# Two sets of PSUM banks for the FFNs' output projections, the attention's weight ring carried on into w_out, and FFN 2's two plain tiles taken block by block: a decoder layer in fp32 on one core

## Chip, cores and metric

The kernel runs on one core of a Trainium2 chip. The metric is the device time of one execution in microseconds (us). Five engines work side by side, each through its own list of instructions in order: TensorE (PE: matmul; PEld is its weight load), VectorE (DVE), ScalarE (ACT), GpSimd (POOL) and SyncE (SP), which here only issues loads. Matmuls write to PSUM, of which there are eight banks; DVE and ACT read the banks out.

## The reference, cut to what matters

One layer for 1024 prompt rows and 32 sample rows (8 sequences of 4), all in fp32, D = 1024, D_FF = 2816:

```python
x = x + 0.5 * gate1 * swiglu_ffn(mod(norm(x)), ffn1_w_in, ffn1_w_out)
x = x + gate2 * (sig(g_A) * DiffAttn(h) + sig(g_B) * Retention(h)) @ w_out     # h = mod(norm(x))
x = x + 0.5 * gate3 * swiglu_ffn(mod(norm(x)), ffn2_w_in, ffn2_w_out)
y = rms_norm(x)
# swiglu_ffn(h, w_in, w_out): a, b = split(h @ w_in);  (silu(a) * b) @ w_out
```

The outputs are y, the keys and values of the attention, and the retention states. Keys, values and states of the sample rows' past are read from a paged cache.

## The kernel before

**Layout.** x lies transposed in SBUF, eight tiles (k = 0 to 7) of 128 features by 1056 rows. The rows go in three blocks of 352 (`RB`; block index `rb`); the last block ends with the 32 sample rows. An fp32 product is made of three matmuls (`mm3`, L239 to L244): each operand is split into a rounded part h, by ACT (L183), and a rest l, by DVE (L193) or, where `eng` is `G`, by POOL (L191); then h·h (L242), h·l (L243) and l·h (L244) are added in one bank. hh[k] and hl[k] are the two parts of the normed, modulated x; a "unit" (`unit_g`, L246) is one 128-column tile of a weight times one block of rows: 8 x 3 matmuls into one bank.

**Weights.** Class `W` (L200) is a ring: `raw` tiles for what is loaded (`load`, by SP), and `parts` pairs of h and l tiles (`out`). `get` (L218) loads, takes a pair and splits. A load waits until the last reader of its raw tile is done, a split until the last matmul on its pair.

**PSUM.** `psum(mm, aux, big)` (L130) hands out the banks: with (3, 3, 1) three banks rotate under the tag "mm" (`mm_ps`, the units), three under "aux" (`aux_ps`), and a double one is "big".

**What sets the order.** The program is written as generators that are woven together (`weave`, L268, with `step` tying a side step behind the main matmul named last). A planner then sorts each engine's instructions before the run, by its own estimate of when each is ready, the earlier in the program first; on the chip an engine goes through its list in that order. Loads stand in SP's list, stores and some loads in POOL's.

**The stages**, in order of time: FFN 1 in (two forms, below), FFN 1 out, retention, differential attention with gates, w_out, FFN 2 in, FFN 2 out with the last norm.

*FFN in.* The first column tiles of w_in are done plainly (`ffn_plain`, L484): for each tile and block a unit for a and one for b, silu by ACT, a product by DVE (L500), a store of the gate product to `gd`. The order is written out at L488: `lead` tiles go together, block by block. FFN 1 has three plain tiles with lead 2, FFN 2 two with lead 1. After block (0, 0) FFN 2 runs `final()` (L1553): the norm of the third block (L438 to L465), which writes hh and hl, then the closing of pools and the room for the sums. From then on `sums` (L514) makes sums of quarters of hh and hl on DVE and ACT. The other tiles take seven products instead of eight (`ffn_seven`, L548) on 4 x 4 blocks of h and w_in; their weights are loaded two tiles of 128 columns at a time, and sums of them are split ahead, at most five (`AHEAD`) before use. FFN 1 uses the ring `W(lower, 2, 4)` (L732) for all of this and for its projection, FFN 2 the ring `w3 = W(last, 3, 3)` (L1529).

*FFN out* (`ffn_out`, L632). w_out's rows go in chunks of two or four 128-row tiles; for each, output tile o and block rb, `one` (L659) multiplies into a bank and DVE adds the result to x (the residual, L475; L480 and L482 for the sample rows). In the last chunk the block is the outer loop (L686), and each block, once done, is normed (`after1`, L809, with `rsqrt_s`, L356, whose sums take an "aux" bank) or, in FFN 2, normed, transposed and stored (`after2`, L1566, whose tiles ym and yt take "mm" banks). In FFN 1 the first units of the retention follow.

*Attention and w_out.* From L1223 on the weights of the attention and of the gates go through `w = W(left, 2, 2, G)`, opened behind the pool "gates" and closed with it. `to_wout` (L1462) runs the gates of head 7 (two weights, three blocks: six units), writes the merged branches to `md`, closes the pools (L1479), opens `w2 = W(xs2, 2, 3)` in their place and a tile for x, loads x again, and does the units of w_out for blocks 0 and 1, woven with `da_sample` (L1073), the attention of the sample rows. The third block of w_out, which needs the sample rows, follows in the loop at L1540, with two norms in between (L1547).

Of the kernel before, what the change touches and what calls it, by code (L numbers as in the profile page):

```python
# [20 lines left out]
P = 128  # L21
# [84 lines left out]
def build(tc, i):  # L106
    nc = tc.nc
    V, S, T, G = nc.vector, nc.scalar, nc.tensor, nc.gpsimd
# [39 lines left out]
    def aux_ps(name):  # L148
        return banks[0][1].tile([P, 512], F32, tag="aux", name=name, bufs=banks[0][3])
# [136 lines left out]
    with tc.tile_pool(name="init", bufs=1) as ip:  # L286
        vec = ip.tile([P, P], F32, name="vec")
        o = 0
# [343 lines left out]
    def ffn_out(w, tp, x, wout, gt, after, chunks, reload, bridge=iter(()), more=iter(())):  # L632


        def parts(t, ci, q):
            return t[(4 if ci % 2 == 0 else 0) + q]

        def stage(ci):
            for q, ft in enumerate(chunks[ci]):
                if ci == 0:  # L640
                    for c in range(2):
                        r = w.p.tile([P, 8, P], F32, tag="wr", name=f"gr{ft}{c}", bufs=w.raw)[:].rearrange("p k c -> p (k c)")[:, :HR]
                        ld(out=r, in_=gd[ft][:, c * HR:(c + 1) * HR])
                        split(*half(4 + 2 * q + c, 0), r)
                else:
                    r = tp.tile([P, ROWS], F32, tag="gr", name=f"gr{ft}", bufs=2)
                    ld(out=r[:], in_=gd[ft][:, :])
                    split(parts(hh, ci, q)[:], parts(hl, ci, q)[:], r[:])
                yield

        assert len(chunks[0]) == 2
        run(stage(0))
        for ci, fs in enumerate(chunks):
            f0, nf = fs[0], len(fs)
            cw = 1024 // nf
            rows = wout[f0 * P:(f0 + nf) * P, :]
            nxt = stage(ci + 1) if ci + 1 < len(chunks) else iter(())

            def one(wt, o, rb):  # L659
                p_ = aux_ps(f"po{ci}_{o}_{rb}")  # L660
                cc = (o * P) % cw
                ws = [(wt[0][:, q, cc:cc + P], wt[1][:, q, cc:cc + P]) for q in range(nf)]
                if ci == 0:
                    c, s = divmod(rb, 2)
                    mm3(p_[:, :QR], ws, [tuple(t[4 + 2 * q + c][:, s * QR:(s + 1) * QR] for t in (hh, hl)) for q in range(nf)])
                    residual_at(tp, x, o, rb * QR, QR, p_, gt())
                else:
                    mm3(p_[:, :RB], ws, [tuple(parts(t, ci, q)[:, rbs(rb)] for t in (hh, hl)) for q in range(nf)])
                    residual(tp, x, o, rb, p_, gt())

            if ci < len(chunks) - 1:
                for ct in range(nf):
                    step(more)
                    wt = w.get(rows[:, ct * cw:(ct + 1) * cw], nf, cw, f"wo{ci}_{ct}")
                    if ci == 0 and ct == 0:
                        reload()
                    for o in range(ct * cw // P, (ct + 1) * cw // P):
                        for rb in range(4 if ci == 0 else NRB):
                            one(wt, o, rb)
                        if o % 2:  # L680
                            next(nxt, None)
                run(nxt)
            else:
                wts = [w.get(rows[:, ct * cw:(ct + 1) * cw], nf, cw, f"wo{ci}_{ct}") for ct in range(nf)]
                todo = iter(())
                for rb in range(NRB):  # L686
                    for o in range(KT):
                        one(wts[o * P // cw], o, rb)
                        if rb == NRB - 1 and o == BO:
                            step(bridge)  # L690
                        if o == 2:
                            step(todo)
                    if rb == NRB - 1:
                        run(bridge)
                    todo = after(tp, rb)
                    next(todo)
                run(todo)
# [34 lines left out]
    w = W(lower, 2, 4)  # L732
    bridge = []
    with ExitStack() as sc, ExitStack() as sb_:
# [28 lines left out]
        w2 = W(sc, 1, 1)  # L763
# [456 lines left out]
                               scalar=subg[:], in1=rr, op0=ALU.mult, op1=ALU.mult)  # L1220


    with ExitStack() as left, ExitStack() as right:  # L1223
        gp = pool(left, "gates")
        w = W(left, 2, 2, G)
        up = pool(left, "dau")
        cosd = up.tile([P, ROWS], F32, name="cosd")
        sind = up.tile([P, ROWS], F32, name="sind")
# [230 lines left out]
        right.close()  # L1459
        psum(3, 3, 1)  # L1460

        def to_wout():  # L1462
            def merged(n0, n1):
                for n_ in range(n0, n1):
                    rb, k = divmod(n_, KT // 2)
                    n = SC if rb == NRB - 1 else RB
                    rc = slice(rb * RB, rb * RB + n)
                    for j in range(2):
                        split(hh[2 * k + j][:, rc], hl[2 * k + j][:, rc], ms[n_][:, j, :n])
                    if len(ms) < NRB * KT // 2:  # L1470
                        mload()

            w.eng = WE
            for n, _ in enumerate(gates(7)):
                if n in MC:
                    merged(MC.index(n), MC.index(n) + 1)
                yield
            merged(len(MC), 4)
            left.close()  # L1479
            w2 = W(xs2, 2, 3)  # L1480
            xp = pool(xs2, "x2")
            X = xp.tile([P, KT, ROWS], F32, name="Y")
            x.extend(X[:, k, :] for k in range(KT))
# [13 lines left out]
            for o in range(1, KT):  # L1497
                order += [(o, 0), (o - 1, 1)]
            for j, (o, rb) in enumerate(order + [(KT - 1, 1)]):
                if rb == 0:  # L1500
                    ws[o] = w2.get(w_out[:, o * P:(o + 1) * P], 8, P, f"wo{o}")
                p_ = yield from unit_g(ws[o], rb, f"wop{o}_{rb}")
                residual(None, x, o, rb, p_, mods[5])
                yield
                if j in (0, 8):
                    merged(4 if j == 0 else 8, 8 if j == 0 else 12)
                if j in XL:
                    xload(XL.index(j) + 1, p_[:, :1])
# [16 lines left out]
            mload()  # L1525
        weave(to_wout(), da_sample(sd), RATIO)
        sx.close()
        X, w = wo
        w3 = W(last, 3, 3, side="right")  # L1529
        tp2 = pool(last, "t2", side="right")  # L1530
        tp = pool(tail, "wo", side="right")
        V.tensor_tensor(out=ors[:], in0=ors[:], in1=gbs[:], op=ALU.mult)
# [7 lines left out]
        for n, o in enumerate((5, 6, 7, 0, 1, 2, 3, 4)):  # L1540
            if n > 2:
                w.eng = G if n in NG else None
                ws[o] = w.get(w_out[:, o * P:(o + 1) * P], 8, P, f"wo2{o}")
            p_ = unit(ws[o], 2, f"wop{o}_2")
            residual(tp, x, o, 2, p_, mods[5])
            if n in (NN, NN + 2):
                run(norm(tp, X, (n - NN) // 2, mods, 7, 6))  # L1547
                keep((n - NN) // 2)
# [4 lines left out]
        def final():  # L1553
            yield from norm(tp, X, 2, mods, 7, 6)
            keep(2)
            tail.close()
            xs2.close()
            gx.extend(quarters(xs3))
            gx.append(pool(tas, "ta", side="right"))


    with last:
        with ExitStack() as s2:
# [39 lines left out]

            todo = back()
            win2 = i["ffn2_w_in"][0]
            ffn_plain(w3, tp2, win2, [0, 1], 1, {(0, 0): final()}, todo)
            for _ in todo:
                pass
            psum(0, 0, 1, True)
# [43 lines left out]
```

## Time and profile before

| | us |
|---|---|
| runs, median of 3 (lowest to highest) | 3100.89 (3099.73 to 3101.14) |
| the profiled execution, its own time | 3098.73 |
| its span, first to last instruction | 3097.0 |
| PE busy | 2963.5 |
| DVE busy | 1969.6 |
| ACT busy | 1319.7 |
| mean granted clock of PE | 0.986 of full speed |

Times of single instructions and waits are read from the one profiled execution, from the start of its span. In it the stages lie about so: FFN 1 in to 585, its projection to 872, retention and attention to 2170, w_out to 2342, FFN 2 in to 2812, its projection to the end. A matmul's duration is modelled; matmuls overlap, so the step from one start to the next is what a stream of them costs. An engine's idle time counts only where the end depends on it.

### The profile page before, as it was taken

Reading aid. Unit: us, or ns where it says so; the run is one execution under the profiler, and the core shown is the slowest. Engines: PE = TensorE matmul, PEld = TensorE weight load, DVE = VectorE, ACT = ScalarE, POOL = GpSimd, SP = SyncE. Lnnn points to the kernel's source line nnn. Section 1 sums busy time; section 2 is a strip of 40 time slices with the busy share of each in tenths; the row PEclk is TensorE's granted clock in tenths of the full one; section 3 lists DMA queues with packets and bytes.
Section 4 is the critical chain, followed back from the end, with each engine's and each line's share of the span. In section 5 each row is a group of like instructions: output and inputs, shape, how many; then the busy total and the mean of one; then the engine's idle time right before and its main releaser. Section 6 shows DMA issues by size and latency. Waiting matters only on the chain.

```text
span 3097.0 us, 51415 instructions
## 1 busy us (share of the span) xinstructions
PE 2963.5 (96%) x20167; PEld 2831.4 (91%) x20167; DVE 1969.6 (64%) x3823; ACT 1319.7 (43%) x2580; POOL 542.6 (18%) x722
## 2 busy tenths in 40 slices
PE   6999999999999999999999999998998999999998
PEld 2899999999999999988899999987898999999998
DVE  4875666665566666667667777665558655556547
ACT  5554444422234343346556556544444433333112
POOL 2200000000132322312233332332023000000002
PEclk8999999999999999999999999999999999999999
DMA  7144343643121322223222121225641222226321
GB/s 278 52 134 121 116 121 119 217 153 114 65 90 62 103 78 81 91 73 114 67 67 64 60 80 57 76 74 171 204 151 47 76 83 76 77 74 218 97 63 57
DMA packets 278732, 319.29 MB, mean 103 GB/s; under 512 B 15568, under 2 KB 224049, under 8 KB 278490
## 3 DMA queue, kind: packets, MB, share of 16 engines
q1 hardware_dynamic: 253418, 232.83, 24.5%
q0 software_dynamic: 25072, 83.18, 7.4%
q8 instruction: 158, 2.59, 0.4%
q14 instruction: 84, 0.69, 0.1%
HBM read 240.00 MB, written 75.96 MB: 102 GB/s over the span
## 4 chain that ended last, share of the span: by engine, by line
PE 33%; DVE 9%; issue 4%; DMA 4%; ACT 3%; POOL 2%; ACTq 0%; DVEq 0%; POOLq 0%; SPq 0%
PE x L244 3%; PE x L242 2%; PE x L243 2%; PE po L242 2%; PE po L243 2%; PE po L244 2%; DVE mx L1328 1%; PE q L242 1%; PE q L243 1%; PE q L244 1%; PE gp L242 1%; ACT P L1330 1%; PE gp L244 1%; PE gp L243 1%; DMA gr<-gd 1%
## 5 line engine op out<-in xcount | busy, mean ns | idle before, releaser
L242 PE MATMUL x<-hh,c 128*128 128x264 f32 x624 | 179.0, 287 | 2.6 <-ACT hh L183 1.6
L244 PE MATMUL x<-hh,c 128*128 128x264 f32 x624 | 178.2, 286 | 1.5 <-DVE c L193 1.5
L243 PE MATMUL x<-hl,c 128*128 128x264 f32 x624 | 179.0, 287 | 0.2 <-DVE hl L193 0.2
L193 DVE TENSOR_TENSOR c<-s,c 128x512 fp32r<-128x512 f32 x156 | 107.7, 691 | 111.4 <-ACT c L183 108.5
L242 PE MATMUL x<-gh,c 128*128 128x264 f32 x624 | 178.2, 286 | 0.0
L243 PE MATMUL x<-gl,c 128*128 128x264 f32 x624 | 177.6, 285 | 0.0
L244 PE MATMUL x<-gh,c 128*128 128x264 f32 x624 | 177.3, 284 | 0.0
L1330 ACT ACTIVATE P<-s,mx 128x256 f32<-128x256 f32 (+7 forms) x128 | 94.2, 739 | 138.4 <-DVE mx L1328 127.6
L475 DVE SCALAR_TENSOR_TENSOR Z<-po,mod,Z 128x352 f32<-128x352 f32 (+3 forms) x176 | 96.5, 554 | 83.7 <-PE po L244 83.3
L475 DVE SCALAR_TENSOR_TENSOR X<-po,mod,X 128x352 f32<-128x352 f32 (+3 forms) x152 | 83.0, 551 | 89.2 <-PE po L244 89.2
L625 POOL DMA_DIRECT2D gd<-p x39 | 21.2, 543 | 649.0 <-DVE p L620 649.0
L242 PEld LDWEIGHTS x<-hh,c 128*128 128x128 f32 x624 | 118.7, 190 | 3.8 <-ACT hh L183 1.8
L244 PEld LDWEIGHTS x<-hh,c 128*128 128x128 f32 x624 | 118.8, 191 | 1.8 <-DVE c L193 1.7
L242 PEld LDWEIGHTS x<-gh,c 128*128 128x128 f32 x624 | 117.4, 188 | 2.4
L243 PEld LDWEIGHTS x<-hl,c 128*128 128x128 f32 x624 | 118.6, 190 | 0.5 <-DVE hl L193 0.4
L243 PEld LDWEIGHTS x<-gl,c 128*128 128x128 f32 x624 | 117.3, 188 | 0.9
L244 PEld LDWEIGHTS x<-gh,c 128*128 128x128 f32 x624 | 117.4, 188 | 0.2
L183 ACT ACTIVATE c<-s 128x512 fp32r<-128x512 f32 x156 | 97.6, 626 | 42.1 <-PE y L244 24.5
L242 PE MATMUL po<-hh,wo_0h 128*128 128x352 f32 (+1 forms) x328 | 104.5, 319 | 4.9 <-DVE X L475 4.7
L242 PE MATMUL po<-hh,wo_1h 128*128 128x352 f32 (+1 forms) x328 | 104.8, 320 | 2.9 <-DVE rs L480 1.2
L183 ACT ACTIVATE hh<-gr 128x1056 fp32r<-128x1056 f32 (+1 forms) x48 | 47.5, 1010 | 133.5 <-DMA gr<-gd 66.8
L243 PE MATMUL po<-hl,wo_0h 128*128 128x352 f32 (+1 forms) x328 | 103.7, 316 | 0.0
(1445 smaller groups left out, 11187.2 us busy)
## 6 DMA issues: line engine op xcount, KB each, us to landing
gr<-gd SPq DMA_DIRECT2D x40, 528.0 KB
gd<-u POOLq DMA_DIRECT2D x39, 264.0 KB, 2.6
gd<-p POOLq DMA_DIRECT2D x39, 264.0 KB, 2.3
ada_0r<-ada_w SPq DMA_DIRECT2D x18, 512.0 KB
ada_1r<-ada_w SPq DMA_DIRECT2D x18, 512.0 KB
ada_2r<-ada_w SPq DMA_DIRECT2D x18, 512.0 KB
ada_3r<-ada_w SPq DMA_DIRECT2D x18, 512.0 KB
st<-state_ret SPq DMA_DIRECT2D x32, 256.0 KB
```

The costliest lines, as they stand in the source:

```text
L183: S.activation(out, in_, AF.Copy, scale=scale)
L193: (eng or V).tensor_tensor(out=l, in0=src, in1=f(h), op=ALU.subtract)
L242: T.matmul(out, wh, xh, start=first and j == 0, stop=False, **kw)
L243: T.matmul(out, wh, xl, start=False, stop=False, **kw)
L244: behind[0] = T.matmul(out, wl_, xh, start=False, stop=last and j == n - 1, **kw).ins
L475: V.scalar_tensor_tensor(out=x[k][:, c0:c0 + n], in0=p_[:, :n], scalar=gt[:, k, 0:1], in1=x[k][:, c0:c0 + n], op0=ALU.mult, op1=ALU.add)
L625: st(out=gd[ft][:, :HR], in_=p1[:])
L1328: V.tensor_reduce(out=mx[:, :n], in_=sv[:, :, :wd], op=ALU.max, axis=AX.X, negate=True)
L1330: S.activation(pr[c][:, :wd], sv[:, j, :wd], AF.Exp, bias=mx[:, j:j + 1], accum_out=sums[c][:, qb:qb + 1])
```

## The change

`one` takes an "mm" bank for odd o and an "aux" bank for even o, in both FFNs. The ring w of the attention is opened ahead of the pool "gates", so that it lies below it, and is closed only in `final()`. Its tiles serve w_out: the first weight is loaded and split at step 9 of the last head's gates, and each later one by a new function `column`, which takes its raw tile from w and its pair from w, or for every third from w2, now a ring of no raw tile and one pair. w3 has two raw tiles and four pairs in place of three and three, and FFN 2's plain tiles go with lead 2: (tile, block) = (0,0), (1,0), (0,1), (1,1), (0,2), (1,2).

```diff
@@ -657,7 +657,7 @@
             nxt = stage(ci + 1) if ci + 1 < len(chunks) else iter(())
 
             def one(wt, o, rb):
-                p_ = aux_ps(f"po{ci}_{o}_{rb}")
+                p_ = (mm_ps if o % 2 else aux_ps)(f"po{ci}_{o}_{rb}")
                 cc = (o * P) % cw
                 ws = [(wt[0][:, q, cc:cc + P], wt[1][:, q, cc:cc + P]) for q in range(nf)]
                 if ci == 0:
@@ -1220,9 +1220,10 @@
                                scalar=subg[:], in1=rr, op0=ALU.mult, op1=ALU.mult)
 
 
+    ring = ExitStack()
+    w = W(ring, 2, 2, G)
     with ExitStack() as left, ExitStack() as right:
         gp = pool(left, "gates")
-        w = W(left, 2, 2, G)
         up = pool(left, "dau")
         cosd = up.tile([P, ROWS], F32, name="cosd")
         sind = up.tile([P, ROWS], F32, name="sind")
@@ -1459,6 +1460,13 @@
         right.close()
         psum(3, 3, 1)
 
+        def column(o, n, name):
+
+            raw = w.load(w_out[:, o * P:(o + 1) * P], 8, P, name)
+            h, l = (wo[1] if n % 3 == 2 else w).out(8, P, name)
+            split(h[:], l[:], raw[:], eng=w.eng)
+            return h, l
+
         def to_wout():
             def merged(n0, n1):
                 for n_ in range(n0, n1):
@@ -1474,10 +1482,12 @@
             for n, _ in enumerate(gates(7)):
                 if n in MC:
                     merged(MC.index(n), MC.index(n) + 1)
+                if n == 9:
+                    ws[0] = w.get(w_out[:, :P], 8, P, "wo0")
                 yield
             merged(len(MC), 4)
             left.close()
-            w2 = W(xs2, 2, 3)
+            w2 = W(xs2, 0, 1)
             xp = pool(xs2, "x2")
             X = xp.tile([P, KT, ROWS], F32, name="Y")
             x.extend(X[:, k, :] for k in range(KT))
@@ -1497,8 +1507,8 @@
             for o in range(1, KT):
                 order += [(o, 0), (o - 1, 1)]
             for j, (o, rb) in enumerate(order + [(KT - 1, 1)]):
-                if rb == 0:
-                    ws[o] = w2.get(w_out[:, o * P:(o + 1) * P], 8, P, f"wo{o}")
+                if rb == 0 and o:
+                    ws[o] = column(o, o, f"wo{o}")
                 p_ = yield from unit_g(ws[o], rb, f"wop{o}_{rb}")
                 residual(None, x, o, rb, p_, mods[5])
                 yield
@@ -1525,8 +1535,8 @@
             mload()
         weave(to_wout(), da_sample(sd), RATIO)
         sx.close()
-        X, w = wo
-        w3 = W(last, 3, 3, side="right")
+        X = wo[0]
+        w3 = W(last, 2, 4, side="right")
         tp2 = pool(last, "t2", side="right")
         tp = pool(tail, "wo", side="right")
         V.tensor_tensor(out=ors[:], in0=ors[:], in1=gbs[:], op=ALU.mult)
@@ -1540,7 +1550,7 @@
         for n, o in enumerate((5, 6, 7, 0, 1, 2, 3, 4)):
             if n > 2:
                 w.eng = G if n in NG else None
-                ws[o] = w.get(w_out[:, o * P:(o + 1) * P], 8, P, f"wo2{o}")
+                ws[o] = column(o, n - 1, f"wo2{o}")
             p_ = unit(ws[o], 2, f"wop{o}_2")
             residual(tp, x, o, 2, p_, mods[5])
             if n in (NN, NN + 2):
@@ -1555,6 +1565,7 @@
             keep(2)
             tail.close()
             xs2.close()
+            ring.close()
             gx.extend(quarters(xs3))
             gx.append(pool(tas, "ta", side="right"))
 
@@ -1603,7 +1614,7 @@
 
             todo = back()
             win2 = i["ffn2_w_in"][0]
-            ffn_plain(w3, tp2, win2, [0, 1], 1, {(0, 0): final()}, todo)
+            ffn_plain(w3, tp2, win2, [0, 1], 2, {(0, 0): final()}, todo)
             for _ in todo:
                 pass
             psum(0, 0, 1, True)
```

## Rows read from the trace of the kernel before

**Rows 1.** The page, its first line and part 1: busy time of each engine, its share of the span, and instructions.

```profile
span 3097.0 us, 51415 instructions
PE 2963.5 (96%) x20167; PEld 2831.4 (91%) x20167; DVE 1969.6 (64%) x3823; ACT 1319.7 (43%) x2580; POOL 542.6 (18%) x722
```

**Rows 2.** The table of engines by stretch: start and end of the stretch, its length, busy us of PE, PEld, DVE, ACT and POOL (with instructions), granted clock of PE, share and rate of the DMAs. The second half of the last chunks of FFN 1's output projection; the end of the gates and the start of w_out; the seven products of FFN 2.

```profile
810.00:872.00 62.00, 55.69 (x328) 53.59 (x327) 42.63 (x80) 29.84 (x58) 19.92 (x20) 0.97 0.23 76
2179.00:2198.00 19.00, 13.59 (x64) 12.11 (x63) 9.13 (x23) 8.16 (x20) 0.71 (x1) 0.73 0.77 244
2430.00:2812.00 382.00, 382.00 (x3131) 382.00 (x3130) 204.56 (x390) 149.58 (x321) 20.08 (x37) 1.00 0.27 84
```

**Rows 3.** The timeline of DVE in FFN 1's last chunk: start, us, engine, line, operation, out<-in, count. L456 is the norm's, L475 the residual, L436 the norm's sum of squares.

```profile
835.25 2.26 DVE L456 SCALAR_TENSOR_TENSOR nt<-X,mod,rrn 128x352 f32<-128x352 f32 x3
...
843.26 1.56 DVE L475 SCALAR_TENSOR_TENSOR X<-po,mod,X 128x352 f32<-128x352 f32 x3
...
848.03 0.52 DVE L436 TENSOR_TENSOR acc<-acc,sq 128x352 f32<-128x352 f32 x1
```

**Rows 4.** Who PE waited for from 585 to 872 us (FFN 1's output projection): us in total, times, longest us.

```profile
PE po L242 <- DVE X L475: 4.7, 2, 4.2
PE po L242 <- DVE rs L480: 2.0, 2, 1.3
PE rsn L359 <- POOL acc L436: 0.8, 1, 0.8
```

**Rows 5.** The table of engines by stretch, columns as in rows 2, for three pieces with a lowered clock.

```profile
843.50:846.90 3.40, 3.01 (x10) 3.01 (x11) 2.44 (x5) 1.85 (x4) 2.34 (x3) 0.50 0.33 121
...
2181.50:2184.90 3.40, 3.40 (x16) 3.26 (x15) 0.73 (x2) 0.85 (x2) 0.71 (x1) 0.50 1.02 295
...
2188.40:2195.10 6.70, 5.76 (x22) 5.12 (x23) 3.56 (x8) 2.66 (x6) 0.00 (x0) 0.50 0.74 230
```

**Rows 6.** The timeline of PE, its last matmuls for the gates.

```profile
2169.84 0.32 PE L243 MATMUL gp<-hl,g_0h 128*128 128x352 f32 x1
2170.00 0.32 PE L244 MATMUL gp<-hh,g_0l 128*128 128x352 f32 x1
```

**Rows 7.** Who PE waited for from 2812 to 3057 us (FFN 2's output projection).

```profile
PE po L242 <- DVE Z L475: 1.3, 3, 0.6
PE po L242 <- DVE rs L480: 0.4, 1, 0.4
```

**Rows 8.** Who PE waited for from 3057 to 3097 us (the tail).

```profile
PE yt L1588 <- ACT yo L1591: 2.2, 3, 1.8
```

**Rows 9.** What writes or reads the tile wo0r: engine, operation, count, ns min/median/max, first and last start.

```profile
L211 SPq DMA_DIRECT2D wo0r<-w_out x1: 395/395/395, 2181.2 to 2181.2; - x1
L183 ACT ACTIVATE wo0h<-wo0r x1: 1041/1041/1041, 2187.9 to 2187.9; 128x1024 fp32r<-128x1024 f32 x1
L193 DVE TENSOR_TENSOR wo0l<-wo0r,wo0h x1: 1226/1226/1226, 2189.0 to 2189.0; 128x1024 fp32r<-128x1024 f32 x1
```

**Rows 10.** The timeline of SP, which issues loads: start, us to issue, line, out<-in, count.

```profile
2179.15 0.33 SPq L1126 DMA_DIRECT2D vp<-cache_v  x1
...
2181.83 0.42 SPq L1126 DMA_DIRECT2D vp<-cache_v  x1
```

**Rows 11.** Who PE waited for from 2170 to 2300 us (w_out and the sample attention).

```profile
PE wop L242 <- ACT wo0h L183: 3.0, 1, 3.0
PE kpt L1132 <- DMA kp<-cache_k: 2.1, 1, 2.1
PE spa L1152 <- DVE sdm L1148: 1.1, 3, 0.5
PE wop L244 <- DVE wo0l L193: 0.3, 1, 0.3
```

**Rows 12.** Who PE waited for from 2341 to 2430 us (FFN 2's plain tiles and the first seven products).

```profile
PE pa L243 <- POOL hl L462: 3.0, 2, 2.4
PE x L242 <- ACT hh L183: 1.6, 1, 1.6
PE x L244 <- DVE c L193: 1.5, 1, 1.5
PE x L242 <- DVE silu L500: 0.7, 1, 0.7
```

**Rows 13.** The timeline of DVE around the last norm before FFN 2. L436 is its sum of squares, L519 and L520 are sums for the seven products, L193 is a split.

```profile
2349.78 0.53 DVE L436 TENSOR_TENSOR acc<-acc,sq 128x352 f32<-128x352 f32 x1 [2.73 <-ACT sq L435]
...
2364.09 0.69 DVE L519 TENSOR_TENSOR t<-hh 128x528 f32<-128x528 f32 x1
2364.71 0.70 DVE L520 TENSOR_TENSOR t_0u<-hl 128x528 f32<-128x528 f32 x1
...
2369.03 1.23 DVE L193 TENSOR_TENSOR wb1l<-wb1r,wb1h 128x1024 fp32r<-128x1024 f32 x1 [2.39 <-ACT wb1h L183]
```

**Rows 14.** The timeline of SP, one of FFN 2's first loads.

```profile
2291.51 0.37 SPq L211 DMA_DIRECT2D wb1r<-ffn_w_in  x1
```

**Rows 15.** The timeline of DVE, in w_out's third block.

```profile
2303.39 0.58 DVE L475 SCALAR_TENSOR_TENSOR Y<-wop,mod,Y 128x352 f32<-128x352 f32 x1 [3.23 <-PE wop L244]
```

**Rows 16.** The table of engines by stretch, columns as in rows 2, for the seven products of FFN 1.

```profile
195.00:585.00 390.00, 390.00 (x3083) 374.11 (x3083) 231.76 (x405) 177.73 (x363) 18.43 (x34) 1.00 0.40 123
```

**Rows 17.** The timeline of DVE, in the first tiles of FFN 2's seven products. L572 is a sum of weight blocks.

```profile
2423.45 0.69 DVE L572 TENSOR_TENSOR s<-wa4r 128x512 f32<-128x512 f32 x1 [0.25 <-DMA wa4r<-ffn_w_in]
```

## The prediction, made before the changed kernel ran

> **What bounds it now.** I read the page first: TensorE (PE) is busy for 2963.5 of 3097.0 us [rows 1], so only its idle time, and time at a low clock, can be won; VectorE (DVE) at 64% matters where it makes PE wait. Next the table of engines by stretch [rows 2]: both seven-product stretches of the FFNs leave PE no gap (FFN 2's: 382.00 of 382.00), while PE is idle for 6.3 us of the end of FFN 1's output projection, for 5.4 us (at a mean clock of 0.73) where the gates give way to w_out, and two plain tiles of FFN 2 hold a wait of their own. Then, for each of these, who PE waited for. The diff touches all three, and only them and the projection of FFN 2.
>
> **The change part by part.** The sum is made against the profiled execution, 3098.73 us around a span of 3097.0; the median of the runs, 3100.89, lies 2.16 above it.
>
> *Six banks in FFN 1's projection.* From 835.25 to 843.26 DVE works on the first block's norm, and the three residuals that hold the three banks run only at 843.26 [rows 3]; PE waits 4.2 us for them in one piece, and 4.7 + 2.0 = 6.7 us for residuals in the stretch [rows 4]. Behind the long wait PE runs at a granted clock of 0.50, its lower level (1.2 GHz), for 3.01 us of work [rows 5], half of which, 1.5 us, is lost. So 6.7 + 1.5 = 8.2 us at most. A unit of the last chunk is 12 matmuls, 0.16 us from start to start [rows 6], so 1.9 us; three more banks carry PE another 5.7 us, past the 4.2. The 1.3 us wait I leave in place: the retention's first units, which already run on PE around it, take the "mm" banks that odd outputs now hold too. I take 8.2 - 1.3 = 6.9 us. Below: nothing is won if PE only comes sooner to the sum of squares of the next block, whose last addition on DVE ends at 848.55 [rows 3] whatever PE does.
>
> The page "TensorE: Matmul & The Clock Gate" of the Trainium skill, section "HAM oscillation — how this bites in real kernels", reports a kernel in which doubling the PSUM buffers brought no further gain (126.6 to 125.5 us). By it this term and the next would be near zero and the sum 8.6 us smaller; the 4.2 us wait for a bank in [rows 4] speaks against it here, and it is the first rival.
>
> *Six banks in FFN 2's projection.* Waits for residuals are 1.3 + 0.4 = 1.7 us [rows 7]; all of it is covered by one or two more units, which are six matmuls, 0.95 us, or more here. I take 1.7. In the tail the transposes of y use the "mm" banks that odd outputs now take as well. What is there now is 2.2 us of waits for an eviction [rows 8]; the cost is between 0 and another 2.2, and I take 0, since these waits end with ACT's eviction itself, late behind the norm of y, and not with a bank for an output.
>
> *w_out's first weights.* wo0 is now loaded at step 9 of the last gates, through the ring that is open anyway. What moves: one load on SP's queue, one ACT rounding (1.04 us), one DVE subtraction (1.23 us) [rows 9]. Today the load is issued at 2181.2 [rows 9], and SP's list is held meanwhile: a load of values goes out at 2179.15, the next one at 2181.83 [rows 10]. With the ring the load's tile is free from the gates' last split on, the h and l tiles when the gates' first weight has done its last unit, and the last gate matmul of all starts at 2170.00 [rows 6]; so wo0, whose subtraction now starts at 2189.0 [rows 9], would be ready some 15 us sooner, and wo1 soon after 2172. PE then has units to put into its waits: 3.0 (wo0h), 2.1 (keys of the sample attention) and 0.3 (wo0l) [rows 11], 5.4 us. It also runs at 0.50 in two pieces there, 3.40 and 5.76 us of work [rows 5], which costs 1.7 + 2.9 us. Together 10.0 us; without the 2.1 and the slow piece behind it, 6.2. An order that is fixed ahead will not always have a unit at hand, as other waits of the sample attention in the same view show (1.1 us [rows 11]); I take 7.0, nearer the low end. Behind the moved steps on ACT and DVE stand splits of the sample attention: at worst 1.2 us later, where PE has w_out to do. X now lies on other freed tiles; its first half is asked for while gates still finish, and has until the first residual. Nothing counted. The number of raw, h and l tiles that w_out cycles through stays 2, 3 and 3, so its later loads are not moved.
>
> *Two plain tiles by blocks.* Today the third block of the first tile waits 3.0 us in all for the last norm's POOL subtraction [rows 12]. In the new order tile 1's first two blocks lie ahead of it, four units of 24 matmuls, 4 x 3.8 = 15 us of PE work, so this wait goes: 3.0 us. It needs wb1 split before PE comes to it. Today its split is at 2369.03, as the third weight tile pair frees late [rows 13]; with four pairs it follows its load, now issued at 2291.51 [rows 14], so near 2300, where DVE is idle for 3.23 us [rows 15]. Free, then; without that cover, 1.2 us on DVE in the norms. Late next: the sums for the seven products, 44 operations of 528 columns by 0.6 to 0.7 us, some 29 us of DVE work, which begin when the last norm ends, at 2364.09 [rows 13]. PE's 0.7 + 1.5 + 1.6 = 3.8 us of waits at the seven products' start come of it [rows 12]; DVE loses the 1.2 us split and the 2.39 us idle before it [rows 13], so DVE and PE move up about alike. I leave the 3.8 where they are; bounds -3.8 to +3.8.
>
> *Two raw tiles instead of three* for FFN 2. FFN 1 runs its seven products and its projection from a ring of two raw and four parts: PE busy 390.00 of 390.00 us [rows 16], and among its projection's waits none for a weight [rows 4]. In both stages the products that PE still has ahead cover a load; the projection's first four loads of gate products queue on SP for two tiles, not three, as they do in FFN 1. I count nothing; the bound below is the second rival's price.
>
> Sum: 6.9 + 1.7 + 7.0 + 3.0 = 18.6 us, giving 3080.1 against the profiled execution, 3082.3 on the scale of the median. All terms at their best: 8.2 + 1.7 + 10.0 + 3.0 + 3.8 = 26.7, so 3074. The weak end of the forecast, w_out 6.2 and half of the rest, 12 us, 3089.
>
> **The rivals.**
> 1. *More banks win nothing.* PE runs ahead, then stands at the matmuls of the second block's sum of squares, whose input DVE ends at 848.55 all the same. For: PE does these where the order puts them, and waited 0.8 us at one already [rows 4]. Against: at 848 there are outputs and retention units that need no norm. 18.6 - 8.6 = 10.0 us: 3090.9.
> 2. *Two raw tiles starve FFN 2's seven products* (the other side). A column tile's second load waits for the last reader of the one before. It is seen once today: DVE stands at 2423.45 for the landing of wa4 [rows 17], and PE waits 1.6 us for what DVE does next [rows 12]. Were that so in each of 20 tiles, 20 x 1.6 = 32 us: 3114. It turns the result slower from 18.6 / 20 = 0.93 us a tile. Against: [rows 16], the same ring with other work beside it.
> 3. *The sample attention sets the end* of its stretch, and w_out's units, done sooner, leave PE idle later in it. Then w_out gives 1 or 2 of its 7.0 us: 3088.
> 4. *The second tile isn't ready*: wb1's split is planned behind the last norm, on DVE from 2349.78 to 2364.09 [rows 13]. PE stands for some 14 us and 1.2 more, and gains no 3.0: 18.6 - 3.0 - 15.5 = 0.1, so 3101. This is also how the edit would fail to do what it says: program order binds PE only through such waits.
>
> **How the numbers follow.** Chances: forecast 0.62, rival 1 0.14, rival 3 0.09, rival 4 0.08, rival 2 0.07. A difference of 0.2%, 6.2 us, is about what a measurement of this kernel can tell from none; faster thus means under 3094.7. The forecast and rivals 1 and 3 lie there but for their tails (0.06): 0.79. Within 0.2%: rival 4 and most of these tails, 0.12. Slower: rival 2 and what is worse than any case here, 0.09. The range runs from 3073, all terms at their best, to 3096, which takes in rivals 1 and 3 with a margin for both together; rivals 2 and 4 and the tails are left out.
>
> **What would show it.** Right: no wait of PE for a residual above 1 us in FFN 1's projection, clock 1.00 there; wo0's split before 2172 and no wait for it; all of tile 1's first block on PE before the third block, and no wait for the norm's subtraction. Wrong: PE idle at a sum of squares' matmul in FFN 1; a wait for a weight in FFN 2's seven products; a long idle time between the first two plain tiles; new low-clock pieces during the sample attention.

## The result, and the profile of the changed kernel

The changed kernel takes 3081.67 us (median of 5 runs, 3076.16 to 3089.97) against 3101.14 us. The medians differ by 19.5 us; the ratio of the two sets of runs, with its 95% interval, is 0.9942 [0.9928, 0.9957], which is 18.0 us (13.3 to 22.3). The forecast was 18.6. The total is right, but three of its four terms were not, and that their errors cancel is luck.

The page's first lines, in place of [rows 1]: PE has 8.4 us less busy time for the same 20167 matmuls (less of it at half clock, a granted clock of 0.50), and the span is 22.6 us shorter.

```profile
span 3074.4 us, 51401 instructions
PE 2955.1 (96%) x20167; PEld 2827.7 (92%) x20167; DVE 1969.2 (64%) x3823; ACT 1319.1 (43%) x2580; POOL 544.1 (18%) x722
```

This profiled execution is the fastest of its five runs (3076.16 us), 5.5 us under their median. So the difference of the two traces is not the effect of the change, and no part is sized below from these two alone.

**FFN 1's projection.** Who PE waited for from 585 to 862 us, in place of [rows 4]:

```profile
PE rsn L359 <- POOL acc L436: 1.9, 1, 1.9
PE adap L414 <- DVE mod L393: 1.0, 1, 1.0
PE rv L242 <- ACT nt L468: 0.6, 1, 0.6
```

No wait for a residual is left: 6.7 us of them are gone. In their place PE stands 1.9 us at the second block's sum of squares, and there are two waits that were not among those of before: 0.6 us behind it, at the retention's first products, and 1.0 us long ahead of it, at 600.8, for `mod` (modulation factors that are computed beside the projection), near where before waits for two of the residuals (0.4 us at 589.4 and 0.8 at 605.4). DVE, POOL and PE around the 1.9 us, in place of [rows 3] (first fence DVE, second POOL and PE):

```profile
832.39 2.26 DVE L456 SCALAR_TENSOR_TENSOR nt<-X,mod,rrn 128x352 f32<-128x352 f32 x3
...
840.42 1.56 DVE L475 SCALAR_TENSOR_TENSOR X<-po,mod,X 128x352 f32<-128x352 f32 x3
...
845.05 0.51 DVE L436 TENSOR_TENSOR acc<-acc,sq 128x352 f32<-128x352 f32 x1
```

```profile
843.28 1.10 POOL L436 TENSOR_TENSOR acc<-acc,sq 128x352 f32<-128x352 f32 x1 [1.05 <-ACT sq L435]
844.43 0.86 PE L359 MATMUL rsn<-acc,ones 128*128 128x352 f32 x2 [1.90 <-POOL acc L436]
```

The three residuals still run behind the first block's norm (840.42, was 843.26); POOL's last addition follows them at 843.28, and PE's matmul at 844.43. From the start of L456 to the end of DVE's last addition it is 13.17 us (832.39 to 845.56); before it was 13.30 (835.25 to 848.55 in [rows 3]). So this chain on DVE is as long as it was. The table of engines by stretch, columns as in [rows 2]: first two rows of before, from 829 us and from 831.86 (which is as far ahead of L456 there as 829 is in after), then after: a half-clock piece in place of the first row of [rows 5], and 829 to 860 us.

```profile
829.00:860.00 31.00, 26.79 (x153) 25.67 (x152) 25.13 (x42) 18.82 (x36) 10.07 (x10) 0.94 0.14 48
831.86:862.86 31.00, 26.20 (x152) 25.20 (x150) 27.41 (x46) 18.66 (x38) 10.05 (x9) 0.94 0.13 47
```

```profile
846.00:849.40 3.40, 3.40 (x12) 3.13 (x11) 2.89 (x5) 1.53 (x4) 0.94 (x1) 0.50 0.27 96
829.00:860.00 31.00, 28.49 (x164) 27.25 (x163) 30.26 (x57) 20.68 (x41) 12.26 (x12) 0.94 0.13 47
```

DVE is busy for 30.26 of 31 us, where it was 25.13 in the same stretch of time and 27.41 in the same stretch of work: with six banks PE no longer waits for a residual here, and DVE has next to no time left.

**w_out.** The tile wo0r, in place of [rows 9]; who PE waited for from 2159 to 2295 us, in place of [rows 11]; and a stretch in which w_out has begun, to set beside the two lower rows of [rows 5].

```profile
L211 SPq DMA_DIRECT2D wo0r<-w_out x1: 384/384/384, 2072.5 to 2072.5; - x1
L183 ACT ACTIVATE wo0h<-wo0r x1: 1043/1043/1043, 2155.0 to 2155.0; 128x1024 fp32r<-128x1024 f32 x1
L193 DVE TENSOR_TENSOR wo0l<-wo0r,wo0h x1: 1215/1215/1215, 2156.5 to 2156.5; 128x1024 fp32r<-128x1024 f32 x1
```

```profile
PE sc L242 <- ACT kth L183: 2.6, 2, 2.5
PE spa L1152 <- DVE sdm L1148: 0.9, 3, 0.5
PE spa L1152 <- ACT hh L183: 0.5, 1, 0.5
PE spa L1152 <- ACT vnh L183: 0.2, 1, 0.2
```

```profile
2176.00:2198.00 22.00, 20.92 (x143) 18.65 (x142) 14.44 (x45) 11.20 (x30) 1.53 (x2) 1.00 0.72 219
```

wo0's split ends at 2157.7, not at 2190; the waits for wo0h, wo0l and the keys are gone. One of 2.5 us for kth (the split of the sample attention's keys) stands at 2172.1, where [rows 11] have none; an earlier one for kth, 2.3 us at 2160.8 before, is 1.0 us at 2151.6 now. The stretch shown is at full clock; most other kernels with the ring have one half-clock piece here (below).

**FFN 2's plain tiles.** Who PE waited for from 2309 to 2424 us, in place of [rows 12], and after it the loads of the second tile's second weight, in place of [rows 14] (its second use, at 2273.4 us, is the one here):

```profile
PE rsn L359 <- DVE acc L436: 4.3, 2, 3.5
PE x L242 <- DVE silu L500: 1.1, 1, 1.1
PE x L244 <- DVE c L193: 0.8, 1, 0.8
PE x L242 <- ACT u L612: 0.6, 1, 0.6
PE x L242 <- ACT hh L183: 0.6, 1, 0.6
...
```

The first line is not new. Its longest wait, 3.5 us, stands in w_out's last part, and before has it ahead of [rows 12], from 2300 to 2341 us:

```profile
PE rsn L359 <- DVE acc L436: 3.6, 1, 3.6
```

The loads:

```profile
L211 SPq DMA_DIRECT2D wb1r<-ffn_w_in x2: 368/368/368, 33.5 to 2273.4; - x2
L183 ACT ACTIVATE wb1h<-wb1r x2: 1057/1060/1062, 44.5 to 2278.1; 128x1024 fp32r<-128x1024 f32 x2
L193 DVE TENSOR_TENSOR wb1l<-wb1r,wb1h x2: 1210/1217/1224, 50.8 to 2279.2; 128x1024 fp32r<-128x1024 f32 x2
```

No wait for the norm's POOL subtraction is left, and wb1 is split 90 us sooner than in [rows 13], at 2279.2; some 20 of these are the kernel's being ahead as a whole. The waits at the seven products' start are 1.1 + 0.8 + 0.6 us at the places that had 0.7 + 1.5 + 1.6; one of 0.6 us, for u, is new.

**FFN 2's projection and the tail.** Who PE waited for from 2788 to 3033, in place of [rows 7], and from 3033 to the end, in place of [rows 8]:

```profile
PE po L244 <- DVE wo_0l L193: 0.5, 1, 0.5
```

```profile
PE yt L1599 <- ACT yo L1602: 3.5, 3, 1.8
PE ym L1592 <- POOL accf L436: 2.2, 1, 2.2
PE ym L1592 <- DVE accf L436: 0.7, 1, 0.7
```

The residual waits (1.7 us) are gone; the tail's waits total 6.4 us. Before, the same view of the tail (3040 us to the end) has 3.8: the 2.2 of [rows 8], and two lines that stand behind it in that view and that the forecast did not count:

```profile
...
PE ym L1581 <- POOL accf L436: 1.3, 1, 1.3
PE yt L1588 <- DVE rs L480: 0.3, 1, 0.3
```

### The profile page after: what moved, and what is told of

It is laid out like the page before. It is cut to its first block, busy times and chain, and to the rows that moved or that the text cites. A ratio compares the mean times of both kernels' runs of the same rounds, so it can differ in the third digit from the quotient of the medians.

```text
span 3074.4 us, 51401 instructions
## 1 busy us (share of the span) xinstructions
PE 2955.1 (96%) x20167; PEld 2827.7 (92%) x20167; DVE 1969.2 (64%) x3823; ACT 1319.1 (43%) x2580; POOL 544.1 (18%) x722
## 4 chain that ended last, share of the span: by engine, by line
PE 35%; DVE 7%; issue 4%; ACT 3%; DMA 3%; POOL 1%; SPq 0%; DVEq 0%; ACTq 0%; POOLq 0%
PE po L244 3%; PE po L242 3%; PE po L243 3%; PE x L242 2%; PE x L243 2%; PE x L244 2%; PE q L243 1%; PE q L242 1%; PE q L244 1%; PE gp L242 1%; PE gp L244 1%; PE gp L243 1%; ACT P L1331 1%; DVE mx L1329 1%; DMA m<-md 1%
## 5 line engine op out<-in xcount | busy, mean ns | idle before, releaser
L193 DVE TENSOR_TENSOR c<-s,c 128x512 fp32r<-128x512 f32 x156 | 107.6, 690 | 111.1 <-ACT c L183 107.0
L475 DVE SCALAR_TENSOR_TENSOR Z<-po,mod,Z 128x352 f32<-128x352 f32 (+3 forms) x176 | 96.5, 554 | 87.3 <-PE po L244 86.6
L475 DVE SCALAR_TENSOR_TENSOR X<-po,mod,X 128x352 f32<-128x352 f32 (+3 forms) x152 | 82.0, 549 | 85.6 <-PE po L244 85.5
L243 PE MATMUL po<-hl,wo_1h 128*128 128x352 f32 (+1 forms) x328 | 104.2, 318 | 0.0
L244 PE MATMUL po<-hh,wo_1l 128*128 128x352 f32 (+1 forms) x328 | 103.8, 318 | 0.0
```

The costliest lines, as they stand in the source:

```text
L193: (eng or V).tensor_tensor(out=l, in0=src, in1=f(h), op=ALU.subtract)
L243: T.matmul(out, wh, xl, start=False, stop=False, **kw)
L244: behind[0] = T.matmul(out, wl_, xh, start=False, stop=last and j == n - 1, **kw).ins
L475: V.scalar_tensor_tensor(out=x[k][:, c0:c0 + n], in0=p_[:, :n], scalar=gt[:, k, 0:1], in1=x[k][:, c0:c0 + n], op0=ALU.mult, op1=ALU.add)
```

## The experiments

Each ratio is against the kernel before, run beside it on the same chip. On that scale the changed kernel is at 0.9942 [0.9928, 0.9957].

**Each part alone, on the kernel before.** p_banks has the first hunk of the diff, p_ring the ring's hunks, p_plain the last two below, p_w3 only the first of these.

```diff
-        w3 = W(last, 3, 3, side="right")
+        w3 = W(last, 2, 4, side="right")
-            ffn_plain(w3, tp2, win2, [0, 1], 1, {(0, 0): final()}, todo)
+            ffn_plain(w3, tp2, win2, [0, 1], 2, {(0, 0): final()}, todo)
```

> The kernel before with the first edit alone: odd outputs of both FFN output projections take an mm bank. Theory A (the prediction's terms): 6.9 + 1.7 = 8.6 us are won, about 3092. Theory B (as the trace of the changed kernel reads): the wait for a bank goes, but PE now stands some 2 us at the second block's sum of squares in FFN 1, with half clock behind it, and the tail of FFN 2 gains nothing; 4 to 6 us in FFN 1 less 0 to 2 us in FFN 2, about 3096. Rival 1 (more banks win nothing): 3101, no difference.

> The kernel before with the ring edit alone: w_out's weights through the ring of the attention, the first one at step 9 of the last gates; single set of banks, FFN 2's plain tiles one after the other, its ring 3 raw and 3 pairs. Theory A (the prediction's term): 7.0 us, about 3094. Theory B (as the trace of the changed kernel reads, where the last norm's sum of squares moves from 4.6 to 19.2 us ahead over this stage): 12 to 15 us, about 3088. Rival 3 (the sample attention sets the end): 1 to 2 us, about 3099.

> The kernel before with the plain tiles' edit alone: FFN 2's ring has 2 raw tiles and 4 pairs, its two plain tiles go block by block. Theory A (the prediction's term): 3.0 us, about 3098. Theory B (as the trace of the changed kernel reads, where the seven products start 3.5 us and run at full clock 5.7 us further ahead than the last norm): 4 to 6 us, about 3096. Rival 4 (second tile not ready): no difference or slower. Rival 2 (two raw tiles starve the seven products): up to 32 us slower, less the 3.0.

> The kernel before with one number pair alone: FFN 2's ring has 2 raw tiles and 4 pairs in place of 3 and 3; the two plain tiles still one after the other. Theory A (the prediction): no cost, and no gain but for the second plain weight's split, which may come before the last norm: 3101, within 2 us. Rival 2 (two raw tiles starve the seven products): 0.93 us and more a tile, 20 us or more slower, up to 3133.

The us of the table are worked out from the ratios.

| kernel | ratio | us against before (3100.07) | forecast term |
|---|---|---|---|
| p_banks | 0.9979 [0.9969, 0.9988] | -6.5 (-9.6 to -3.7) | -8.6 |
| p_ring | 0.9982 [0.9971, 0.9994] | -5.6 (-9.0 to -1.9) | -7.0 |
| p_plain | 0.9979 [0.9970, 0.9988] | -6.5 (-9.3 to -3.7) | -3.0 |
| p_w3 | 0.9990 [0.9981, 1.0000] | -3.1 (-5.9 to 0.0) | 0 |

The first three lines add up to 18.6 us; against 18.0 for the whole no interaction shows, within intervals of some 3 us each. Rival 1 in full (banks win nothing) lies outside p_banks's interval; between 8.6 us and theory B's 4 to 6, less 0 to 2, that interval does not decide. Rival 3 (1 to 2 us) is at the edge of p_ring's. p_plain's leaves out the 3.0 of theory A. Theory B of p_ring, read from the two traces alone, was wrong: 12 to 15 us against 5.6. Rival 2 falls with p_w3. Its 370 us of seven products have PE busy for all of them, with two raw tiles:

```profile
2430.00:2800.00 370.00, 370.00 (x3035) 370.00 (x3034) 197.41 (x374) 141.40 (x306) 19.46 (x36) 1.00 0.25 80
```

Its interval reaches from -5.9 to 0; whether it is faster at all, and why, these runs do not settle.

**The changed kernel again, and with one thing undone.**

> The changed kernel once more, beside the kernel before on the same chip. Theory A: the change is worth about 18 us (the sum of the three parts measured alone, 6.5 + 5.6 + 6.5 = 18.6), so 3080 to 3083 as a median; the 3076.16 of the profiled run was one with few low-clock pieces. Rival: the combination is worth more than its parts, as the profiled run reads (22 us and more): under 3078.

after2: 0.9936 [0.9920, 0.9951], 3080.82 us: the sum of the parts, theory A. The rival, that the whole is worth more than its parts, came from the one fast profile.

a_noring is the changed kernel without the ring's hunks, a_lead1 has `lead` back at 1.

> The changed kernel without the ring edit: w_out's weights through a ring of their own that opens when the gates are done, as before. Theory A (the prediction's term and the stage read over eleven profiles, 232 us without and 224 with the ring from the retention's last transposes to w_out's last product): 7 to 8 us slower than the changed kernel, 3088. Theory B (the ring alone measured 5.6 us against the kernel before; the rest is chance of the low-clock pieces): 4 to 6 us.

> The changed kernel with FFN 2's two plain tiles one after the other again (its ring stays at 2 raw tiles and 4 pairs). Theory A (the prediction's term): the wait for the last norm's POOL subtraction is back, 3.0 us slower than the changed kernel. Theory B: the term is 5 to 6 us, since the waits in this stage also bring half-clock pieces, 1.7 us each (8 of them in the four profiles without the paired order, 1 in the six with it, from the last unit of w_out to the end of the seven products' first tiles): about 3086.

a_noring: 0.9960 [0.9946, 0.9973], so against the changed kernel's two ratios the ring is worth 5.6 to 7.4 us (each of these to some 6 us, which does not decide between the theories). In it PE waits for wo0h again, 5.0 us in one piece, and the clock is 0.50 around it, from 2182.3 to 2189.1. a_lead1: 0.9965 [0.9953, 0.9977]; the paired order is worth 7.1 to 9.0 us, each again to some 6 us. That leans to theory B, and the stages below decide for it. The waits of a_lead1 from 2320 to 2425 us, and its engines by stretch there, a half-clock piece first:

```profile
PE pa L243 <- POOL hl L462: 3.6, 2, 3.0
PE x L244 <- DVE c L193: 1.5, 1, 1.5
PE x L242 <- ACT hh L183: 0.7, 1, 0.7
...
```

```profile
2356.50:2363.30 6.80, 5.94 (x20) 5.94 (x21) 0.50 (x3) 2.03 (x4) 0.81 (x1) 0.50 0.00 0
2417.90:2421.30 3.40, 3.40 (x18) 3.40 (x17) 2.47 (x6) 1.18 (x3) 0.54 (x1) 0.50 0.20 80
```

Behind the 3.0 us wait PE does 5.94 us of work at half clock, which is 3.0 us lost, and 1.7 more at 2417.9.

**Is it the early request or the open ring?** a_late drops the request at step 9.

```diff
-                if n == 9:
-                    ws[0] = w.get(w_out[:, :P], 8, P, "wo0")
-                if rb == 0 and o:
+                if rb == 0:
                     ws[o] = column(o, o, f"wo{o}")
```

> The changed kernel without the early request at step 9 of the last gates: w_out's first weight is asked for like the others, at its first unit, through the ring that is already open. Theory A (the free tiles of the open ring are what counts; loads sort by when a tile is free): within 2 us of the changed kernel, no wait of PE for wo0h. Theory B (the place of the request counts): the wait of 3 us for wo0h and a low-clock piece come back, 3 to 7 us slower.

0.9924 [0.9909, 0.9939], not slower: theory A. Its tile wo0r shows why. The load goes out at 2077.8 without being asked for early, since the ring's raw tile is free and the planner sorts by that:

```profile
L211 SPq DMA_DIRECT2D wo0r<-w_out x1: 383/383/383, 2077.8 to 2077.8; - x1
L183 ACT ACTIVATE wo0h<-wo0r x1: 1043/1043/1043, 2160.6 to 2160.6; 128x1024 fp32r<-128x1024 f32 x1
```

**What holds FFN 1's end now?** a_sq4 puts the second block's sum of squares two units later on PE; a_norec relieves DVE: it leaves out the reciprocal in the norms of the first two blocks, which are then scaled by the root itself. (`at` is 4 in FFN 1 and 2 in FFN 2; `rec` is false in `after1` for the first two blocks.)

```diff
-                        if o == 2:
+                        if o == (at if rb == NRB - 1 else 2):
                             step(todo)
```

```diff
-        V.reciprocal(out=r[:, :n], in_=r[:, :n])
+        if rec:
+            V.reciprocal(out=r[:, :n], in_=r[:, :n])
```

> The changed kernel, with the sum of squares of the second block of FFN 1's output put two units later in the last block (behind output 4, not 2). Theory A (rival 1 in part: PE with more banks comes to that matmul before its operand, 1.90 us idle and half clock behind it): the wait goes, 2 to 4 us faster than the changed kernel, 3078. Theory B (that wait hides one that stands behind it: the retention's first products need the norm that follows): the wait comes back at the retention's first products, no difference.

> The changed kernel with less work for DVE where FFN 1's output ends: the reciprocal (2.35 us) is left out of the norms of the first and second block, so these are scaled by the root and not by its inverse. Theory A (with six banks DVE is the bound there: busy 30.3 of the 31 us from 829 to 860, 25.1 before): PE's waits at the second block's sum of squares and at the retention's first products, 1.9 + 0.6 to 2.1 us, shrink by 2 us or more each, and the stage with its low-clock piece gets 2 to 5 us shorter. Theory B (PE's waits there come from the order of its list, not from DVE): the stage changes by less than 1 us.

a_sq4: 0.9933 [0.9918, 0.9947], the same as the changed kernel. PE's waits from 835 to 875 us, first a_sq4, then a_norec:

```profile
PE rv L242 <- DVE rs L480: 3.8, 1, 3.8
```

```profile
PE rv L242 <- DVE rs L481: 1.2, 1, 1.2
```

And DVE in 829 to 860, in the same order:

```profile
829.00:860.00 31.00, 27.56 (x170) 26.84 (x169) 30.97 (x51) 20.00 (x39) 15.80 (x16) 1.00 0.24 82
```

```profile
829.00:860.00 31.00, 29.85 (x183) 28.90 (x182) 29.09 (x62) 20.80 (x43) 13.88 (x13) 1.00 0.14 48
```

With the matmul moved, the wait comes back whole at the retention's first products, and DVE is still full (30.97 of 31). With 2 x 2.35 us less on DVE, PE's waits shrink from 1.9 + 0.6 to 1.2 us, and the stage, from the first product of the projection to the first product of the retention's output (tile pro), takes 348.6 us. The eight profiles with six banks and unchanged norms have 351.3 to 355.5; the 351.3 is the one that, like a_norec's, has no half-clock piece in this stage, so 2.7 us is the fair difference, one profile against one; 0.5 of it lies at the wait for `mod`. The order of PE's list is not the cause; DVE's work is. The reciprocal both fills DVE and lies in the chain that PE waits for, and a_norec does not tell these two apart. In total a_norec (0.9940 [0.9927, 0.9954]) can't be told from the changed kernel: its interval reaches 4 us to either side.

**FFN 2's banks.** a_ffn1 uses six banks in FFN 1 only (first new line), a_chunk also in FFN 2's projection but for its last chunk (second); `both` is true in FFN 1.

```diff
-                p_ = (mm_ps if o % 2 else aux_ps)(f"po{ci}_{o}_{rb}")
+                p_ = (mm_ps if o % 2 and both else aux_ps)(f"po{ci}_{o}_{rb}")
+                p_ = (mm_ps if o % 2 and (both or ci < len(chunks) - 1) else aux_ps)(f"po{ci}_{o}_{rb}")
```

> The changed kernel with FFN 2's output projection back on the aux banks alone. Theory A (the prediction's term): 1.7 us slower than the changed kernel. Theory B (the stages read from the traces, less their low-clock pieces: 263.4 to 265.1 us from the first to the last output product of FFN 2 with one set of banks, 264.3 to 265.9 with both): no difference, or up to 2 us faster than the changed kernel.

> The changed kernel, with both sets of banks in FFN 1 and in all chunks of FFN 2's output but the last, which is on the aux banks alone as before. Theory A (the FFN 2 part wins 1.2 us where waits for residuals were, in the first chunks, and loses 2.6 us in the last, where the last norm's tiles share the mm banks): 2 to 3 us faster than the changed kernel, waits in the tail back to 3.7 us from 6.3, waits for residuals at most 0.5 us. Theory B (the waits in the tail come from something else): tail as in the changed kernel.

a_ffn1: 0.9923 [0.9908, 0.9938], 3077.64 us, not slower than the changed kernel: theory B; a_chunk: 0.9937 [0.9923, 0.9950], 3078.14 us. The waits in the tail of a_chunk:

```profile
PE yt L1599 <- ACT yo L1602: 2.2, 3, 1.8
PE ym L1592 <- POOL accf L436: 1.3, 1, 1.3
PE yt L1599 <- DVE rs L480: 0.3, 1, 0.3
```

They are those of before, to the tenth, and only the last chunk's banks differ from the changed kernel: theory A for the mechanism. Summed over all profiles, the tail's waits (ym and yt) are 6.3 us in each of the eight that use both sets in the last chunk, and 3.9 to 4.1 in the six that do not. From the first product of FFN 2's projection to the end a_chunk takes 282.2 us, the changed kernel 286.6 and 284.9 in its two profiles. These two and a_late have medians 2 to 4 us under the changed kernel's, but no interval is clear of it: no version here is shown to beat it.

**The stages over all fourteen profiles.** The runs of one kernel lie some 10 us apart, so the ratios bound a part only to 3 to 5 us. Stages are sharper: below, the time of PE from one landmark to the next, mean and extremes over the profiles without and with the part, and how much of it the granted clock was 0.50. (a_sq4 and a_norec are left out of the first line, a_chunk of the last.)

| stage (part) | without | with | difference | us at 0.50, without / with |
|---|---|---|---|---|
| FFN 1's projection to the first product of tile pro (six banks) | 357.6, 356.3 to 359.6, n 4 | 353.3, 351.3 to 355.5, n 8 | -4.3 | 5.1 / 3.4 |
| last matmuls of the attention's tile rr to w_out's last product (ring) | 232.1, 231.0 to 233.8, n 5 | 224.8, 220.4 to 226.6, n 9 | -7.3 | 22.2 / 13.6 |
| w_out's last product to FFN 2's projection (paired tiles) | 471.7, 470.3 to 473.1, n 5 | 465.3, 464.3 to 467.1, n 9 | -6.4 | 7.5 / 0.8 |
| FFN 2's projection and tail (six banks) | 283.4, 281.7 to 284.5, n 5 | 284.8, 283.0 to 286.6, n 8 | +1.4 | 14.2 / 15.4 |

In the first three lines the two ranges do not touch; in the last they overlap. In the first line, p_ring alone has 10.2 us at half clock; without it the difference is 3.6. In the third, the kernels without the part hold two with the new ring in the old order, p_w3 and a_lead1 (470.3 and 473.1): the order makes the difference, not the ring. PE's idle time changes by -3.1, -3.0, -2.9 and +1.7 us from line to line. The sum of the differences is -16.6 us, inside both measurements of the whole (-18.0 and -19.9, each to some 5 us).

## Why the prediction came out right, and where it did not

**Six banks in FFN 1's projection: 6.9 forecast, 4.3 measured.** The 4.2 us wait and the others for residuals went as forecast. But of the marks the prediction set, "clock 1.00 there" did not come, and "PE idle at a sum of squares' matmul in FFN 1" did. The step that failed is the one against rival 1, "at 848 there are outputs and retention units that need no norm": there are, but they lie on PE around a norm for which DVE has no time to spare, with 30.26 of 31 us busy. So part of rival 1 happened: of idle time 3.1 us were won and not 5.4. The 1.5 us of half clock counted as won mostly stayed: seven of the eight profiles with six banks (a_sq4 and a_norec apart) have such a piece in this stage, five behind the wait at the sum of squares and two behind the one at the retention's first products. a_sq4 and a_norec show that it is DVE's work and not the order on PE. A second wait was not foreseen either: 0.9 to 3.2 us for `mod`, in all ten profiles with six banks in FFN 1 and in none of the four without. It ends with DVE too; no run relieves it. The Trainium skill ("TensorE: Matmul & The Clock Gate", section "HAM oscillation — how this bites in real kernels") reports a kernel in which double buffering in PSUM brought no further gain. Here the trace agrees in FFN 2 and disagrees in FFN 1, by the 4.3 us.

**Six banks in FFN 2's projection: 1.7 us won by the forecast, 1.4 lost by the stages (not clear of zero).** The waits for residuals went (1.7 us to none; p_banks alone still has 2.0). The failed step is "the cost is between 0 and another 2.2, and I take 0": the tail's waits rose from 3.8 to 6.4 us, 2.6 us, above even that bound. a_chunk ties them to the last chunk's use of the "mm" banks. By the views, 1.6 of the 2.6 end with additions for the norm's sum of squares (2.2 + 0.7 against 1.3), as in FFN 1, and 1.3 with ACT's eviction yo (3.5 against 2.2), less 0.3 that is gone. Whether yt waits for a bank, or PE only reaches ym and yt sooner, no run tells apart.

**w_out's first weights: 7.0 forecast, 7.3 measured.** Right in size, and mostly by the steps named: wo0's split by 2157.7 (forecast: before 2172), no wait for it, nor for the keys. By the table, 8.6 us less at half clock make 4.3 of the 7.3 (the forecast saw 4.6 at most), and idle time the other 3.0 (5.4 at most). The 3.0 + 0.3 us for wo0 are won; the 2.1 us for the keys are not, since in eight of the nine profiles with the ring PE waits 2.2 to 2.7 us for kth there instead. What brings it is the open ring alone; the request at step 9, which the forecast counted as the move, is worth nothing that these runs show. Rival 3's 1 to 2 us are excluded by the stage. Half clock did not quite leave the start of w_out: one piece of 3.4 us remains in seven of the nine profiles with the ring (not in the one shown above), where the five without have two or three, 10.2 to 13.6 us together.

**Plain tiles by blocks: 3.0 forecast, 6.4 measured.** The wait for the norm's subtraction went, as forecast, and rival 4 did not come: wb1 was split at 2279.2. The step that failed is that no half clock was counted here: the forecast priced half clock only where the profile of before had it beside a wait that was to go, and this wait had none there. Over the profiles the stage has 6.7 us less at half clock, some 3.4 us of time, which is the whole miss; the idle time is 2.9 us less, about as forecast. In before's profile the pieces lay behind the waits at the seven products' start (1.5 and 1.6 us in [rows 12]), which the forecast left where they are; they fell to 0.8 and 0.6.

**Two raw tiles: 0 forecast.** There is no wait for a weight in FFN 2's seven products, in p_w3 or in the changed kernel, whose only wait from 2430 to 2788 us is 1.4 us for a product of DVE, 4.5 us ahead of the projection. Rival 2 is out. But this wait is a small price: all eleven profiles with two raw tiles have it, 0.6 to 1.4 us, and the three with three raw tiles have 0.2 us at most. In p_w3 DVE splits the projection's first weight just ahead of that product (2799.82, then 2800.97).

So the misses are -2.6, -3.1, +0.3 and +3.4 us, and they cancel to -2.0. That the sum came out better than its parts is luck.

## What to carry to other kernels

When more buffers free an engine, look at how busy the engine that empties them is in that very stretch, and not at the wait alone: here VectorE had 3.6 of 31 us to spare before and 0.7 after, and new waits took the place of the old. A wait of two or three us on TensorE can be worth about twice its length, because half clock may follow it in one execution and not in the next (1.9 us, with or without 3.4 us at half clock behind it); price it by several profiles. And before loads are moved by hand, open their buffers earlier: where a planner sorts by when a tile is free, that alone moved this load by 100 us.

## What the runs showed of the hardware

The same wait, in two executions of the same kernel. After the 1.9 us wait at FFN 1's sum of squares the changed kernel's first profile runs at half clock, its second (after2) doesn't. The table of engines by stretch, 6.8 us from the end of the wait, first one, then the other:

```profile
844.40:851.20 6.80, 6.77 (x28) 6.07 (x29) 6.29 (x14) 3.49 (x8) 0.94 (x1) 0.75 0.38 134
```

```profile
843.40:850.20 6.80, 6.77 (x38) 6.21 (x39) 6.62 (x14) 3.78 (x8) 0.95 (x1) 1.00 0.38 134
```

PE is busy for 6.77 us in both, but with 28 matmuls in the one (mean granted clock 0.75) and 38 in the other (1.00). The Trainium skill ("TensorE: Matmul & The Clock Gate", section "What's actually happening") says that what watches TensorE's activity runs freely and does not start anew with the kernel. These two rows fit that, but no run here shows it by itself. The spread of the runs goes with the clock. Of the 52 runs of the kernel before that stood beside the experiments (3095.0 to 3108.9 us), the 13 with a mean clock of 0.985 or more have a median of 3098.1 us, the 4 with 0.981 or less 3105.8.
